# FFN up-projection by one Strassen step on token halves, in five passes of 512 tokens

## Chip, cores and metric

The kernel runs on one core of one Trainium2 chip. Its engines are TensorE (PE, matmuls and transposes into PSUM; its weight loads are listed as PEld), VectorE (DVE), ScalarE (ACT), GpSimd (POOL) and SyncE (SP, which issues nearly all DMAs). The metric is the device time of one execution in microseconds (us), as the median of several executions.

## What is computed

One layer of an encoder with parallel mixers, for a sample of 2048 tokens (`s`) and a prompt of 512 tokens (`p`), all in float32. The part that matters here is the feed-forward network (FFN) at its end:

```
h   = rms_norm(x2, norm2_g)                       # [L, 1024]
u   = dwconv3(h @ w_ffn_in, ffn_conv_w, ffn_conv_b)   # [L, 5632], width-3 convolution along the tokens
act = gelu(u[..., :2816]) * u[..., 2816:]         # gate part, up part
y   = x2 + act @ w_ffn_out
```

`x2` is the output of the mixers (attention, pooling, Hyena convolution) and of an output projection with its residual. To keep float32 accuracy on TensorE's faster float32r matmul, each operand is split in two: `hi`, the value rounded by a copy, and `lo`, the remainder. A product is then three matmuls: hi·hi, hi·lo, lo·hi (`mm3`, lines 323 to 325).

## The kernel before

The program has three stretches. First the projections of both batches run with the sample's mixers beside them, and then the sample's output projection (`front`). Then the FFN's up-projection (`ffn_in`) runs with the prompt's mixers beside its first part. Last comes the down-projection (`ffn_out`), with the halves of the weights `wo` that `wo_load` loaded before.

`ffn_in` is called three times: for the first 1024 tokens of the sample, for the 512 tokens of the prompt, and for the other 1024 tokens of the sample. Each call goes over 22 column tiles `f` of the gate part and the up part (`part` 0 and 1). For each part it loads 128 columns of weights (`fw`, 512 KB), splits them (`fwhi` on ACT, line 318; `fwlo` on DVE, line 319), and runs 8 x 3 matmuls of 512 tokens for each 512 tokens into one PSUM bank. ACT then writes the middle tap of the convolution with its bias from PSUM into `cv` (line 1322), and DVE adds the two other taps from PSUM (line 1312). Gelu is on ACT (line 1338), gate times up on DVE (line 1340), and SP stores the result to `act` in DRAM.

`ffn_prep` makes the FFN's input: row tiles of 128 tokens are loaded, normed (ACT, DVE, and a power on POOL, line 346), transposed on PE (line 357), and split into `hi` and `lo`.

`drive` writes two streams of instructions into one program: `main`, here `ffn_in`, and `side`, the mixers of the prompt and `ffn_prep` for the next part. A ratio says how much of the side stream goes with the main one. A scheduler then orders each engine's instructions; on the chip each engine runs its own in that order, and semaphores hold an instruction back until its inputs and buffers are there. In `run` the side stream is: the sample's mixers, its attention, `norm_s` (FFN input of the first half), then, once `front` has ended (`"up"`), the prompt's attention, pooling, Hyena and output projection, and the prompt's FFN input.

Of the kernel before, what the change touches and what calls it, by code (L numbers as in the profile page):

```python
# [32 lines left out]
class Seq:  # L33
    """One request batch: its length, its FFT split N = 64 * N2 and the derived tile counts."""
# [15 lines left out]
# the tables of 128 partitions that stay on chip: name and columns  # L50
# [5 lines left out]
def _shape_tables():  # L56
    """DFT matrices, positions, decays, distances: all from shapes alone."""
# [40 lines left out]
    # of the first four heads; those of the others are 1/16 of it  # L98
# [14 lines left out]
    for s in SEQS.values():  # L113
# [34 lines left out]
        # rows (b, ri, g, j), columns (ri, g, k2), block diagonal over g  # L148
# [13 lines left out]
        # positions of the forward filter and of the backward one, in the order (j, b, n1)  # L162
# [15 lines left out]
        # [b, n1, chunk, g, j, c']  # L178
# [15 lines left out]
def _arrays(inputs):  # L194
    """The arrays of the launch: the large inputs as they are, the small ones laid out by partition."""
# [35 lines left out]
RATIO_P = 0.4  # L231
# [10 lines left out]
class Trunk:  # L242
# [13 lines left out]
    def consts(self, c):  # L256
# [12 lines left out]
        self.edge = c.tile([128, 2, 2 * NF], F32, name="edge")  # L269
# [46 lines left out]
    def split(self, x, hi, lo):  # L316
        nc = self.nc
        self.keep(nc.scalar.activation(hi, x, AF.Copy))  # L318
        self.keep(nc.vector.tensor_tensor(lo, x, hi, op=ALU.subtract))  # L319

    def mm3(self, ps, lhi, llo, rhi, rlo, start, stop):
        nc = self.nc
        nc.tensor.matmul(ps, lhsT=lhi, rhs=rhi, start=start, stop=False)  # L323
        nc.tensor.matmul(ps, lhsT=lhi, rhs=rlo, start=False, stop=False)  # L324
        nc.tensor.matmul(ps, lhsT=llo, rhs=rhi, start=False, stop=stop)  # L325
# [12 lines left out]
    def norm(self, pool, g, x, n):  # L338
        """The first n rows of x after RMS norm with gain g, in place."""
# [10 lines left out]
    def norm_t(self, xn, n, hi, lo, c0, bank):  # L350
        """xn, transposed, to columns c0.. of hi and lo."""
# [13 lines left out]
    def front(self):  # L365
        """p of the sample, q, k and v of both, p of the prompt, then the sample's output projection behind its attention. The
        weights of a part take the place of those of the part before, tile by tile."""
# [5 lines left out]
        with tc.tile_pool(name="front", bufs=1, reuse_waits="tile") as pool:  # L373
# [16 lines left out]
            def fill(i, c0):  # L390
                """Weights i: columns c0.. of w_in, piece by piece."""
# [30 lines left out]
            def place(i):  # L422
                """Where row tile i goes, transposed: hi, lo and the column."""
# [32 lines left out]
            def also(it):  # L456
                """it, with the row tiles and the weights to come."""
# [54 lines left out]
            # the first tiles as they come; the weights last, for the next pool to start below them  # L512
# [1047 lines left out]
```

## Time and profile before

| | us |
|---|---|
| three runs | 3138.93, 3138.91, 3135.88 (median 3138.91) |
| span of the profiled execution | 3140.1 |
| from the first up-projection matmul to the first of the down-projection | 1144.9 to 2531.7 |
| from there to the end | 608.4 |

The profile is of one execution of its own; its time is given as its span, from the first to the last instruction, 1.2 us above the median of the runs. Rows of instruction groups read: line, engine, operation, output and inputs with their shapes, count, then busy time in us and the mean of one in ns, then the engine's idle time before them and who ended it. Matmuls overlap, so their pace is read from how far their starts are apart, not from their durations.

### The profile page before, as it was taken

What the parts mean: (1) busy time and instruction counts of PE and PEld (TensorE: products, weight loads), DVE (VectorE), ACT (ScalarE), POOL (GpSimd) and SP (SyncE); (2) the same over time, 40 slices, a digit from 0 to 9 for tenths busy, and PEclk for the clock granted to TensorE, in tenths of its full rate; (3) what the DMA queues carried; (4) which work ended last, traced back from release to release, by engine and by line L of the source; (5) the groups of instructions that cost most, each with busy time, mean ns of one, the idle gap of its engine ahead of it and who ended that gap; (6) DMA issues with size and microseconds to landing.
All of it is one profiled execution on the core that took longest, in us unless ns stands there. A gap on an engine that the chain in (4) does not pass through costs nothing.

```text
span 3140.1 us, 41553 instructions
## 1 busy us (share of the span) xinstructions
PE 3053.5 (97%) x15992; PEld 2556.1 (81%) x15992; DVE 1676.3 (53%) x3168; ACT 1173.7 (37%) x2021; POOL 210.5 (7%) x248
## 2 busy tenths in 40 slices
PE   7999999899999999999999999999999999999999
PEld 6887888888878877788887888888888888888887
DVE  7443567759998777666445565564444442111111
ACT  5222454448877546434223343332222231111110
POOL 1000000012233230000000000000000000000000
PEclk9999999999999999999999999999999999999999
DMA  5555586663533441454313243442222143223222
GB/s 178 151 152 138 163 230 170 178 176 100 152 100 94 145 138 61 131 166 133 98 63 128 89 137 118 127 142 67 74 67 74 54 131 111 74 77 101 74 75 77
DMA packets 399051, 369.94 MB, mean 118 GB/s; under 512 B 74937, under 2 KB 332857, under 8 KB 397829
## 3 DMA queue, kind: packets, MB, share of 16 engines
q1 hardware_dynamic: 395685, 356.64, 37.6%
q0 software_dynamic: 2880, 10.49, 0.8%
q8 instruction: 126, 2.06, 0.3%
q14 instruction: 72, 0.59, 0.1%
q10 hardware_dynamic: 288, 0.16, 0.0%
HBM read 278.08 MB, written 89.13 MB: 117 GB/s over the span
## 4 chain that ended last, share of the span: by engine, by line
PE 69%; DVE 5%; ACT 3%; DMA 2%; issue 1%; POOL 1%; SPq 0%; POOLq 0%; ACTq 0%; DVEq 0%
PE b L323 21%; PE b L325 21%; PE b L324 21%; PE b L1160 1%; PE b L1111 1%; ACT sb L1127 1%; PE b L1142 1%; PE b L1141 1%; PE b L865 1%; PE b L852 1%; DVE sb L1114 0%; PE b L357 0%; DVE nx L347 0%; DVE sb L1135 0%; DMA raw<-in_w_in_dram 0%
## 5 line engine op out<-in xcount | busy, mean ns | idle before, releaser
L323 PE MATMUL b<-h,fwhi 128*128 128x512 f32 x1408 | 562.5, 400 | 0.9 <-DVE x L1237 0.9
L325 PE MATMUL b<-h,fwlo 128*128 128x512 f32 x1408 | 560.0, 398 | 0.3 <-DVE fwlo L319 0.3
L324 PE MATMUL b<-h,fwhi 128*128 128x512 f32 x1408 | 559.0, 397 | 0.0
L1312 DVE SCALAR_TENSOR_TENSOR cv<-b,cst,cv 128x511 f32<-128x511 f32 (+1 forms) x616 | 351.8, 593 | 153.9 <-ACT cv L1322 147.3
L319 DVE TENSOR_TENSOR fwlo<-fw,fwhi 128x1024 fp32r<-128x1024 f32 x132 | 161.4, 1224 | 326.7 <-ACT fwhi L318 326.7
L325 PEld LDWEIGHTS b<-h,fwlo 128*128 128x128 f32 x1408 | 265.5, 189 | 64.5 <-DVE fwlo L319 0.8
L323 PEld LDWEIGHTS b<-h,fwhi 128*128 128x128 f32 x1408 | 265.8, 189 | 63.1 <-issue 1.8
L324 PEld LDWEIGHTS b<-h,fwhi 128*128 128x128 f32 x1408 | 265.7, 189 | 61.6
L319 DVE TENSOR_TENSOR al<-ar,ah 128x512 fp32r<-128x512 f32 x110 | 76.0, 691 | 420.4 <-ACT ah L318 420.4
L318 ACT ACTIVATE fwhi<-fw 128x1024 fp32r<-128x1024 f32 x132 | 139.8, 1059 | 387.9 <-PE b L324 385.1
L324 PE MATMUL b<-h,ah 128*128 128x512 f32 x640 | 249.2, 389 | 0.0
L323 PE MATMUL b<-h,ah 128*128 128x512 f32 x640 | 249.1, 389 | 0.0
L325 PE MATMUL b<-h,al 128*128 128x512 f32 x640 | 248.9, 389 | 0.0
L318 ACT ACTIVATE ah<-ar 128x512 fp32r<-128x512 f32 x110 | 69.4, 631 | 474.9 <-PE b L324 462.4
L1322 ACT ACTIVATE cv<-b,cst 128x512 f32<-128x512 f32 x220 | 169.2, 769 | 200.1 <-PE b L325 199.9
L323 PE MATMUL b<-W,h 128*128 128x256 f32 (+1 forms) x672 | 224.7, 334 | 2.1 <-ACT W L318 0.7
L324 PE MATMUL b<-W,h 128*128 128x256 f32 (+1 forms) x672 | 214.8, 320 | 0.7 <-DVE W L319 0.3
L325 PE MATMUL b<-W,h 128*128 128x256 f32 (+1 forms) x672 | 213.9, 318 | 0.0
L323 PE MATMUL b<-h,W 128*128 128x256 f32 x640 | 200.3, 313 | 3.4 <-ACT W L318 1.5
L325 PE MATMUL b<-h,W 128*128 128x256 f32 x640 | 184.5, 288 | 3.8 <-DVE W L319 3.8
L324 PE MATMUL b<-h,W 128*128 128x256 f32 x640 | 183.1, 286 | 0.0
L325 PEld LDWEIGHTS b<-h,al 128*128 128x128 f32 x640 | 120.1, 188 | 25.3 <-DVE al L319 0.2
(204 smaller groups left out, 5791.8 us busy)
## 6 DMA issues: line engine op xcount, KB each, us to landing
fw<-in_w_ffn_in_dram SPq DMA_DIRECT2D x132, 512.0 KB, 3.8
ar<-acts SPq DMA_DIRECT2D x88, 256.0 KB, 2.7
nx<-in_x_sample_dram SPq DMA_DIRECT2D x32, 512.0 KB, 4.4
tf<-in_t2f_s_dram SPq DMA_DIRECT2D x64, 256.0 KB, 3.3
acts<-cv SPq DMA_DIRECT2D x22, 512.5 KB, 2.6
raw<-in_w_in_dram SPq DMA_DIRECT2D x44, 256.0 KB, 3.1
rw<-in_w_ffn_out_dram SPq DMA_DIRECT2D x44, 256.0 KB, 2.7
acts<-cv SPq DMA_DIRECT2D x22, 511.5 KB, 3.1
```

The source lines that it names most:

```text
L318: self.keep(nc.scalar.activation(hi, x, AF.Copy))
L319: self.keep(nc.vector.tensor_tensor(lo, x, hi, op=ALU.subtract))
L323: nc.tensor.matmul(ps, lhsT=lhi, rhs=rhi, start=start, stop=False)
L324: nc.tensor.matmul(ps, lhsT=lhi, rhs=rlo, start=False, stop=False)
L325: nc.tensor.matmul(ps, lhsT=llo, rhs=rhi, start=False, stop=stop)
L852: nc.tensor.matmul(ps[:, i * C:i * C + C], lhsT=tf[:, i], rhs=x1[:, k0 + i], start=True, stop=True)
L865: nc.tensor.matmul(ps[:, i * C:i * C + C], lhsT=ti[:, i], rhs=t1[:, i * C:i * C + C], start=True, stop=True)
L1111: nc.tensor.matmul(ps[:, :nk], lhsT=qs[h][:, b * 128:b * 128 + 128], rhs=kk[:, ks], start=(i == 0), stop=(i == 1))
L1127: nc.scalar.activation(sc[h][:, :nk], sc[h][:, :nk], AF.Exp, bias=ng[:, h:h + 1], accum_out=den[:, h:h + 1])
L1141: nc.tensor.matmul(po, lhsT=v, rhs=phi, start=(i == 0), stop=False)
L1312: nc.vector.scalar_tensor_tensor(o, ps, taps[i], o if to is None else to, op0=ALU.mult, op1=ALU.add)
L1322: nc.scalar.activation(cv[:, a - o0:a - o0 + 512], ps, AF.Identity, scale=taps[1], bias=self.fcb[:, m:m + 1])
```

## The change

The up-projection runs in five passes of 512 tokens: four of the sample, then the prompt. In each pass one step of Strassen's algorithm (Winograd's form, with chains of sums) replaces each group of 2 x 2 block products. The blocks are: the first and second half of the 1024 input channels (the depth), the gate and the up columns of tile `f`, and the first and second 256 tokens. Instead of 8 products of half depth there are 7.

The token side is combined once for a pass, in `ffn_prep`: seven operands (`op` 0 to 6) of half depth and 256 tokens, each in `hi` and `lo`, from sums and differences on DVE and POOL. The weight side is combined for every tile `f` of every pass: four sums on POOL (`s12`, `s34`, 128x512 each), and four split groups, `g1` (the gate weights), `g2` (`s12`), `g3` (`s34`) and `g4` (half of the up weights). ACT makes all `hi`; DVE makes the `lo` of `g1` and `g2`, POOL that of `g3` and `g4`. Tile `f` of a pass is called a step below. The buffers of `g1` to `g3` (`fk`) are one set, so those of the next step can only be written when the products of this step have read them.

A step's products go in the order 1 to 7, each of 4 x 3 matmuls of 256 tokens, into four PSUM banks: 1 (`pa`, `g1`), 2 (`pb`, `g2`), 3 (`pd`, `g3`), 4 (`pc`, `g2`), and then 5 (`pa`, `g1`), 6 (`pd`, `g4`) and 7 (`pc`, `g3`), which add to what stands in their banks. Between them ACT copies `pa` to `u` (after 1 and after 5), and DVE makes partial sums `u2`, `u3` and the outputs in `u`, a tile in SBUF with one buffer. Product 5 must wait for the copy of `pa` after product 1, product 6 for `u3`, product 7 for the output from `pc`. The convolution then reads `u` instead of PSUM: middle tap on ACT, the two others as `scalar_tensor_tensor` on DVE (called taps below), gelu on ACT, and gate times up on POOL. The border tokens of two passes go through `edge`.

Beside this, the prompt's output projection loads its weights in two halves of 512 columns and prepares its input for each; the prompt's attention and the first pass's input `prep(0)` stand ahead of `"up"`; `RATIO_P` is 1.0 instead of 0.4; seven instead of eight row tiles of `w_ffn_out` fit each large tile.

```diff
-RATIO_P = 0.4
+RATIO_P = 1.0
+FT = 512
...
-        self.keep(nc.vector.tensor_tensor(lo, x, hi, op=ALU.subtract))
+        self.keep((engine or nc.vector).tensor_tensor(lo, x, hi.bitcast(F32), op=ALU.subtract))
...
+            def put(op, cs, x):
+                self.split(x, h[:, op, 0, :, cs], h[:, op, 1, :, cs], nc.gpsimd if op > 4 else None)
...
+                if i % 2 == 0:
+                    b = [pool.tile([128, 4, 128], F32, tag=f"b{j}", name=f"b{j}") for j in range(2)]
+                    for j in range(2):
+                        nc.scalar.activation(b[j], pv[j], AF.Copy)
+                        put(j, cs, pv[j])
+                else:
+                    nc.vector.tensor_tensor(t1, pv[0], b[0], op=ALU.subtract)
+                    nc.vector.tensor_tensor(t2, pv[1], t1, op=ALU.subtract)
+                    put(2, cs, pv[1])
+                    put(3, cs, t1)
+                    nc.gpsimd.tensor_tensor(b[0], t2, b[0], op=ALU.subtract)
+                    nc.gpsimd.tensor_tensor(b[1], b[1], t2, op=ALU.subtract)
+                    put(4, cs, t2)
+                    put(5, cs, b[0])
+                    put(6, cs, b[1])
...
+            a11, a12, a21, a22 = (x[:, k:k + 4] for x in ws for k in (0, 4))
+            s12, s34 = (pool.tile([128, KD, 128], F32, tag="fs", bufs=2, name="fs") for _ in range(2))
+            g1 = split(ws[0], "fk", 3)
+            nc.gpsimd.tensor_tensor(s12[:, 0:4], a21, a22, op=ALU.add)
+            nc.gpsimd.tensor_tensor(s12[:, 4:8], s12[:, 0:4], a11, op=ALU.subtract)
+            nc.gpsimd.tensor_tensor(s34[:, 0:4], a11, a21, op=ALU.subtract)
+            g2 = split(s12, "fk", 3)
+            nc.gpsimd.tensor_tensor(s34[:, 4:8], a12, s12[:, 4:8], op=ALU.subtract)
+            g3 = split(s34, "fk", 3, nc.gpsimd)
+            g4 = split(a22, "fl", 1, nc.gpsimd)
+            u = pool.tile([128, 2, FT + 4], F32, tag="u", bufs=1, name="u")
...
+            def add(o, ps, x):
+                nc.vector.tensor_tensor(o, ps[:, :N], x, op=ALU.add)
+
+            pa, pb, pd, pc = bank(), bank(), bank(), bank()
+            yield from product(pa, g1, 0, 0)
+            nc.scalar.activation(u[:, 0, lo], pa[:, :N], AF.Copy)
+            yield from product(pb, g2, 4, 4)
+            add(u2, pb, u[:, 0, lo])
+            yield from product(pd, g3, 0, 5)
+            add(u3, pd, u2)
+            yield from product(pc, g2, 0, 3)
+            add(u[:, 1, hi], pc, u3)
+            yield from product(pa, g1, 4, 1, False)
+            nc.scalar.activation(u[:, 0, lo], pa[:, :N], AF.Copy)
+            yield from product(pd, g4, 0, 6, False)
+            add(u[:, 1, lo], pd, u2)
+            yield from product(pc, g3, 4, 2, False)
+            add(u[:, 0, hi], pc, u2)
...
+                nc.scalar.activation(cv, u[:, part, c0:c0 + w], AF.Identity, scale=self.fcw[:, 1, m:m + 1], bias=self.fcb[:, m:m + 1])
+                for i in (0, 2):
+                    nc.vector.scalar_tensor_tensor(cv, u[:, part, c0 + i - 1:c0 + i - 1 + w], self.fcw[:, i, m:m + 1], cv,
+                                                   op0=ALU.mult, op1=ALU.add)
...
-            nc.vector.tensor_tensor(cvs[0], cvs[0], cvs[1], op=ALU.mult)
+            nc.gpsimd.tensor_tensor(cvs[0], cvs[0], cvs[1], op=ALU.mult)
...
-                     self.mark("c", "s"), pace(RATIOS[2]), self.attention(S, *att), norm_s(), self.need("up"), self.attention(P, *att),
+                     self.mark("c", "s"), pace(RATIOS[2]), self.attention(S, *att), self.attention(P, *att), prep(0), self.need("up"),
```

DVE in the up-projection, before (a stretch of the sample's second half; `b0` to `b4` are PSUM banks):

```order
L319 TENSOR_TENSOR fwlo_19637<-fw_19634,fwhi_19636 128x1024
L1312 SCALAR_TENSOR_TENSOR cv_19435<-b2_19466,cst_75,cv_19435 128x511 x2
L1312 SCALAR_TENSOR_TENSOR cv_19435<-b2_19466,cst_75,cv_19435 128x1
L1312 SCALAR_TENSOR_TENSOR cv_19435<-b1_19436,cst_75,cv_19435 128x1
L1312 SCALAR_TENSOR_TENSOR cv_19503<-b3_19504,cst_75,cv_19503 128x511 x2
```

DVE in one step of the second pass of the changed kernel (`fk_21273` and `fk_21280` are the `lo` of the next step's `g1` and `g2`):

```order
L1378 TENSOR_TENSOR u23_21156<-b1_21159,u_21155 128x256
L1378 TENSOR_TENSOR u23_21157<-b2_21160,u23_21156 128x256
L1378 TENSOR_TENSOR u_21155<-b3_21161,u23_21157 128x256
L320 TENSOR_TENSOR fk_21273<-fw_21266,fk_21272 128x1024
L320 TENSOR_TENSOR fk_21280<-fs_21270,fk_21279 128x1024
L1378 TENSOR_TENSOR u_21155<-b2_21160,u23_21156 128x256
L1378 TENSOR_TENSOR u_21155<-b3_21161,u23_21156 128x256
L1410 SCALAR_TENSOR_TENSOR cv_21255<-u_21155,cst_75,cv_21255 128x512
L1410 SCALAR_TENSOR_TENSOR cv_21260<-u_21155,cst_75,cv_21260 128x512
L1410 SCALAR_TENSOR_TENSOR cv_21255<-u_21155,cst_75,cv_21255 128x512
L1410 SCALAR_TENSOR_TENSOR cv_21260<-u_21155,cst_75,cv_21260 128x512
```

The taps took one operand from PSUM before; now both of their tiles, `u` and `cv`, lie in SBUF, and five sums of 256 columns from PSUM stand among them. In some steps beside the preparation of the next pass the `lo` of `g1` stands ahead of the second or third sum.

POOL in the up-projection had nothing before but powers and a few sums for the prompt's mixers and the norms. In the changed kernel this is what stands there for one step (`fs` are `s12` and `s34`, `fl` is `g4`):

```order
L1360 TENSOR_TENSOR fs_21270<-fw_21268 128x512
L1362 TENSOR_TENSOR fs_21271<-fw_21266,fw_21268 128x512
L1361 TENSOR_TENSOR fs_21270<-fs_21270,fw_21266 128x512
L1364 TENSOR_TENSOR fs_21271<-fw_21266,fs_21270 128x512
L1415 TENSOR_TENSOR cv_21118<-cv_21118,cv_21123 128x512
L320 TENSOR_TENSOR fl_21289<-fw_21268,fl_21288 128x512
L320 TENSOR_TENSOR fk_21285<-fs_21271,fk_21284 128x1024
```

Seven operations of two SBUF inputs a step came to POOL: the four sums for the next step, gate times up of the step before, and the `lo` of the next step's `g4` and `g3`.

ACT for the same step (`b0` is bank `pa`; `fk_21272`, `fk_21279`, `fl_21288`, `fk_21284` are the `hi` of the next step's `g1`, `g2`, `g4`, `g3`):

```order
L1383 ACTIVATE u_21155<-b0_21158 128x256
L1397 ACTIVATE u_21155<-edge_78 128x2x2
L319 ACTIVATE fk_21272<-fw_21266 128x1024
L319 ACTIVATE fk_21279<-fs_21270 128x1024
L1391 ACTIVATE u_21155<-b0_21158 128x256
L319 ACTIVATE fl_21288<-fw_21268 128x512
L319 ACTIVATE fk_21284<-fs_21271 128x1024
L1401 ACTIVATE edge_78<-u_21155 128x4
L1408 ACTIVATE cv_21255<-u_21155,cst_75 128x512
L1408 ACTIVATE cv_21260<-u_21155,cst_75 128x512
L1413 ACTIVATE cv_21255<-cv_21255 128x512
L1383 ACTIVATE u_21292<-b0_21295 128x256
```

The four `hi` of the next step stand between the copies of this one and its convolution; the next step's first copy of `pa` (last row) stands behind this step's gelu, and waits for all four taps, since they read the one buffer of `u`.

More of the change, by code (lines that the diff above doesn't have):

```diff
@@ L1256, in out_proj @@
-            yield from self.need((key, n))
-            for t in range(L // 128):
-                ts = slice(t * 128, t * 128 + 128)
-                ca = pool.tile([128, DM], F32, tag="ca", name="ca").rearrange("p (k t) -> p k t", k=KD)
-                nc.sync.dma_start(out=ca, in_=self.cat[n][:, ts].rearrange("(k p) t -> p k t", p=128))
-                x = pool.tile([128, DM], F32, tag="ox", name="ox")
-                nc.sync.dma_start(out=x, in_=src[ts, :])
-                sq, hi, lo = (pool.tile([128, KD, 128], dt, tag=nm, name=nm) for nm, dt in (("osq", F32), ("chi", F32R), ("clo", F32R)))
-                self.out_prep(ca, sq, hi, lo)
-                yield from self.until(self.now + T_NORM)
-                r = self.out_scale(pool, bank, sq, GROUPS)
-                yield from self.out_product(bank, hi, lo, x, r, GROUPS, wo)
-                nc.gpsimd.dma_start(out=self.x2[n][t * 128:t * 128 + 128, :], in_=x)
-                self.done.add(("x2", n, t))
@@ L1446, in big @@
         def big(pool):
-            return pool.tile([128, 2, KD * 1024], F32R, tag="h", name="h")
-        def hview(t):
-            return [t[:, i, :KD * 1024].rearrange("p (k t) -> p k t", k=KD) for i in range(2)]
+            return pool.tile([128, 7, 2, 4, FT // 2], F32R, tag="h", name="h")
         mc = self.ctx.enter_context(tc.tile_pool(name="mconst", bufs=1, side="right", reuse_waits="tile"))
@@ L1462, in run, with prep @@
         att = [att(i) for i in range(3)]
[L1463 to L1478 removed]
+        passes = [(S, t) for t in range(0, S.L, FT)] + [(P, t) for t in range(0, P.L, FT)]
+        pools, hs = [], {}
+        def prep(i):
+            if i < 2:
+                pools.append(self.ctx.enter_context(tc.tile_pool(name=f"h{i}", bufs=1, side="right", reuse_waits="tile")))
+            hs[i] = big(pools[i % 2])
+            yield from self.ffn_prep(passes[i][0], hs[i], passes[i][1], a)
+            self.done.add(("h", i))
         def consts():
@@ L1520, in load @@
         def load():
-            for f, v in enumerate(wviews(big(pb))):
+            po.append(self.ctx.enter_context(tc.tile_pool(name="ffo", bufs=1, side="right", reuse_waits="tile")))
+            for f, v in enumerate(wviews(big(pools[1]))):
                 self.wo_load(v, f, raw)
                 yield 4000
-        self.drive(self.ffn_in(S, pool, cvp, hB, 1024, 1024, self.rotate((0, 1, 2, 3, 4))), load(), 0.1)
-        wctx.close()
+        with tc.tile_pool(name="ffw", bufs=1, reuse_waits="tile") as pool:
+            for i, (s, t0) in enumerate(passes):
+                if i == 0:
+                    side = self.drive(self.ffn_in(s, pool, hs[0], t0, self.rotate((0, 1, 2, 3))), side, RATIO_P)
+                else:
+                    self.wo = {}
+                    ahead = prep(i + 1) if i + 1 < len(passes) else load()
+                    side = self.drive(self.ffn_in(s, pool, hs[i], t0, self.rotate((0, 1, 2, 3))), ahead, 0.1)
+                self.drive(side or (), None, 0)
```

211 lines of the change are left out of this document (105 added, 106 removed).

## The prediction

> **What bounds the kernel now.** I read the busy shares first, then the up-projection by windows, then single operations.
>
> ```profile
> PE 3053.5 (97%) x15992; PEld 2556.1 (81%) x15992; DVE 1676.3 (53%) x3168; ACT 1173.7 (37%) x2021; POOL 210.5 (7%) x248
> ...
> L323 PE MATMUL b<-h,fwhi 128*128 128x512 f32 x1408 | 562.5, 400 | 0.9 <-DVE x L1237 0.9
> L323 PE MATMUL b<-hp,fwhi 128*128 128x512 f32 x352 | 139.7, 397 | 0.0
> ...
> 1144.90:2531.70 1386.80, 1379.36 (x6171) 1116.13 (x6172) 764.13 (x1375) 495.76 (x694) 40.48 (x49) 1.00 0.33 102
> 2200.00:2300.00 100.00, 100.00 (x428) 80.40 (x427) 46.76 (x85) 26.98 (x32) 0.00 (x0) 1.00 0.22 71
> ```
>
> TensorE bounds it. In the up-projection (third row: busy time of PE, weight loads, DVE, ACT, POOL; then clock, DMA share, GB/s) PE has work for 1379 of 1387 us, DVE for 55%, ACT for 36%, POOL for 3%. The pace: 428 matmuls of 512 tokens in 100 us, 0.2336 us each. There are 3 x (1408 + 352) = 5280 of them, so 1233 us; the other 154 us are PE work of the prompt's mixers and of the norms beside it.
>
> **What the change can save.** It needs 5 passes x 22 steps x 7 products x 12 = 9240 matmuls of 256 tokens. The trace has that shape in the input projection:
>
> ```profile
> 101.70 0.28 PE L325 MATMUL b<-h,W 128*128 128x256 f32 x1
> ...
> 102.78 0.28 PE L325 MATMUL b<-h,W 128*128 128x256 f32 x1
> ```
>
> Nine matmuls later the start is 1.08 us later: 0.12 us each, weight load hidden. A product is 12 x 0.12 = 1.44 us, a step 10.1 us, all 110 steps 1109 us. So 124 us, 4% of the kernel, is the most that PE gives.
>
> **What a step asks of the other engines.** Durations:
>
> ```profile
> L318 ACT ACTIVATE fwhi<-fw 128x1024 fp32r<-128x1024 f32 x132 | 139.8, 1059 | 387.9 <-PE b L324 385.1
> L318 ACT ACTIVATE ah<-ar 128x512 fp32r<-128x512 f32 x110 | 69.4, 631 | 474.9 <-PE b L324 462.4
> ...
> L507 ACT ACTIVATE o<-b 128x256 f32<-128x256 f32 x20 | 7.6, 381 | 5.3 <-PE b L325 5.1
> ...
> L319 DVE TENSOR_TENSOR fwlo<-fw,fwhi 128x1024 fp32r<-128x1024 f32 x132 | 161.4, 1224 | 326.7 <-ACT fwhi L318 326.7
> L802 DVE SCALAR_TENSOR_TENSOR hst<-hst,mcst 128x512 f32<-128x512 f32 x12 | 8.8, 737 | 3.8 <-ACT hst L799 3.6
> L926 DVE TENSOR_TENSOR zg<-b,zg 128x256 f32<-128x256 f32 x16 | 5.8, 400 | 0.0
> ...
> L1054 POOL TENSOR_TENSOR kn<-kt,hr 128x512 f32<-128x512 f32 x6 | 6.2, 1040 | 0.5
> L1059 POOL TENSOR_TENSOR qn<-qt,hr 128x1024 f32<-128x1024 f32 x20 | 38.8, 1942 | 53.4 <-issue 26.8 <-PE b L1086 25.1 <-POOL hr L1013 0.7
> ```
>
> DVE: two `lo` of 1.22, four taps of 0.74, five sums of 0.40: 7.4 us. POOL: six operations of 512 at 1.04 and one of 1024 at 1.90 (its duration undisturbed, below): 8.1 us. ACT: three `hi` of 1.06, one of 0.63, two copies of 0.38, and about 2.4 for convolution, gelu and edges: 7.0 us. Each is below 10.1, so by sums alone PE would stay the bound. They are not independent, though:
>
> ```profile
> 782.39 0.69 DVE L319 TENSOR_TENSOR W<-raw,W 128x512 fp32r<-128x512 f32 x1
> ...
> 783.47 2.34 DVE L319 TENSOR_TENSOR W<-raw,W 128x512 fp32r<-128x512 f32 x1
> ...
> 781.63 1.64 POOL L1013 TENSOR_TENSOR hr<-hss,mhalf 128x8 f32<-128x8 f32 x1 [21.52 <-DMA raw<-in_w_in_dram]
> 783.36 1.90 POOL L1059 TENSOR_TENSOR qn<-qt,hr 128x1024 f32<-128x1024 f32 x1
> ...
> 789.80 0.75 DVE L581 SCALAR_TENSOR_TENSOR W<-raw,cst,W 128x512 fp32r<-128x512 f32 x1
> ...
> 790.47 0.95 DVE L581 SCALAR_TENSOR_TENSOR W<-raw,cst,W 128x512 fp32r<-128x512 f32 x1
> ...
> 789.93 0.95 POOL L1209 TENSOR_TENSOR osq<-osq 128x128 f32<-128x128 f32 x1
> ...
> 790.84 0.91 POOL L1209 TENSOR_TENSOR osq<-osq 128x128 f32<-128x128 f32 x1
> ...
> 1487.99 0.75 DVE L1237 SCALAR_TENSOR_TENSOR ox<-b,or,ox 128x512 f32<-128x512 f32 x1 [1.87 <-PE b L325]
> ...
> 1487.15 2.00 POOL L1209 TENSOR_TENSOR osq<-osq 128x256 f32<-128x256 f32 x4
> ```
>
> (Start and duration in us, engine, operation.) The same DVE subtraction takes 0.69 us, and 2.34 when POOL's wide multiplication has begun 0.11 us before it: it ends at 785.81, 0.55 behind POOL's 785.26. So **a DVE operation with two inputs in SBUF and a POOL operation on SBUF exclude each other**. The next four rows show the turns: the POOL sum of 789.93 ends at 790.88, 0.33 behind the first DVE operation; the second DVE operation ends 0.54 behind that; the second sum 0.33 behind that. Where both have work queued, they alternate. In the last two rows the DVE operation reads PSUM and one SBUF tile, beside a running series of POOL sums, and keeps its 0.75 us.
>
> The Trainium skill, page "SBUF — State Buffer", section "Who interferes with whom", states that two SBUF inputs on DVE contend with a GpSimd reader and that the loser waits for the whole instruction. The trace agrees for wide operations; 782.39 stayed at 0.69 us inside a power of 1.64 us on eight columns, so I count the time of reading only. By whole instructions a step would hold 8.1 + 5.4 = 13.5 us, about the loop that I find below, so the sum hardly hangs on it.
>
> Before, the taps read PSUM, and POOL was idle. Now both `lo`, the four taps and all seven POOL operations are of the kind that excludes. Counted behind a release: taps 0.54, `lo` about 1.08, POOL 0.92 and 1.8 (0.12 less, as 0.33 is less than the 0.45 of a free 128-column sum): 4 x 0.54 + 2 x 1.08 + 6 x 0.92 + 1.8 = 11.6 us a step, above PE's 10.1.
>
> **The loop.** By the order of ACT, DVE and POOL, a step is tied to the one before, from the end of its product 5 to that of the next:
> - ACT, in order, for the next step's weights: `g1` 1.06 and `g2` 1.06, the second copy of `pa` 0.38, `g4` 0.63, `g3` 1.06: 4.19 us (`g1` waits for product 5, `g3` for product 7, which has ended by then).
> - POOL: the `lo` of `g4` holds it 0.2 us more, then the `lo` of `g3`: 1.90.
> - Meanwhile the convolution's first tap is ready and waits; then tap, sum, tap, sum, tap, sum, tap, as POOL's four sums are queued there: 0.54 + 3 x (0.92 + 0.54) = 4.92.
> - Only now may ACT write the one buffer `u`: 0.38. Product 5 waits for this copy: 1.44.
> - Some six handovers of 0.05: 0.3.
>
> Sum: 4.19 + 2.1 + 4.92 + 0.38 + 1.44 + 0.3 = **13.3 us a step**. PE stands idle for 3.2 us of it, mostly ahead of product 5. The weights' DMA does not come into it:
>
> ```profile
> fw<-in_w_ffn_in_dram SPq DMA_DIRECT2D x132, 512.0 KB, 3.8
> ```
>
> The second weight tile of the next step is asked for when `g1`'s `lo` is done, and lands 3.8 us later, about when POOL comes to the sums; 1 MB per 13.3 us is 79 GB/s.
>
> **The other terms.**
>
> ```profile
> 307.10:310.60 3.50, 1.59 (x13) 1.42 (x13) 0.37 (x1) 0.00 (x0) 0.00 (x0) 1.00 0.83 254
> 310.60:314.05 3.45, 3.45 (x19) 3.45 (x18) 0.00 (x0) 0.80 (x2) 0.00 (x0) 0.51 0.43 139
> ...
> 1156.20:1159.60 3.40, 0.98 (x8) 0.69 (x7) 3.12 (x7) 0.67 (x2) 2.70 (x3) 1.00 0.36 101
> 1159.60:1163.00 3.40, 3.13 (x15) 2.28 (x14) 2.74 (x6) 2.52 (x4) 2.40 (x2) 1.00 0.45 130
> ...
> 800.00:900.00 100.00, 96.68 (x595) 82.25 (x594) 91.84 (x244) 85.02 (x199) 29.63 (x25) 1.00 0.40 118
> ...
> L1160 PE MATMUL b<-cst,sb x448: 270/272/332, 714.8 to 1279.3; 128*128 128x128 f32 x150
> ...
> L325 PE MATMUL b<-owhi,clo 128*128 128x512 f32 x64 | 25.5, 399 | 0.0
> ```
>
> - *Clock.* After 1.9 idle of 3.5 us the granted clock was 0.51 for the next 3.4 us. After 2.4 idle of 3.4 us at 1156 it stayed 1.00. The gap ahead of product 5 is longer than both, so I take a quarter of 110 gaps at 1.4 us (product 5 at half speed): 40 us, bounds 0 and 150. The Trainium skill, page "TensorE: Matmul & The Clock Gate", section "Why this matters for your kernels", says that gaps up to about 3 us keep the clock. The trace differs, with 0.51 behind 1.9 us; by the page the sum would be 40 us less.
> - *First pass.* The prompt's pooling, Hyena and output projection (3 x 64 matmuls of 0.2336, 45 us of PE) run beside it. They were at most the 154 us above; PE's idle time hides part, while they also use DVE and POOL: 80, bounds 0 and 154.
> - *Input of the next pass, weights of the last.* Four preparations add about 8 us of DVE and 11 us of POOL that exclude each other; 14 splits of `wo` add 10 us: 60, bounds 0 and 100.
> - *Order.* In 18 steps a `lo` stands ahead of a sum that product 6 or 7 waits for, 2.4 or 1 us late: 25, bounds 0 and 45.
> - *Start.* The prompt's attention moves ahead of the first up-projection matmul, with its DMAs and its POOL operations, beside the last sample tiles of the output projection. DVE is at 92% where the sample's attention runs. Now it runs between 1144.9 and 1279.3 (last row but one), so at most 134 us come ahead, at least none, if it fits beside those tiles: 40, nearer to none, since PE work of the output projection is there to run beside it.
> - The down-projection keeps its 608 us: 7 weight tiles ahead of it instead of 8 last 7 x 5.5 = 38 us, and the rest arrive faster than that.
>
> Sum: 110 x 13.3 = 1463, + 40 + 80 + 60 + 25 = 1668 instead of 1387: +281; +40 at the start: **+321**, 3140 to 3461; against the median, 1 us less. I take 3460.
>
> **The rivals.**
> 1. *Exclusion without strict turns.* POOL's sums come late or DVE's taps go in a row; the loop shrinks to what the exclusion itself needs, 11.7 us: 110 x 1.6 = 176 less, **3285**. For it: the second weight tile lands only just in time. Against it: the turns at 789.80.
> 2. *No bound but PE*, the other side: the taps on `u` do not wait for POOL. The loop then fits into PE's 10.1 plus 0.4 for product 3, which waits for `g3`: 110 x 10.5 + 115 for the rest = 1270, -117 + 40: **3060**. It decides in favour of the change below 12 us a step. Against it: 783.47.
> 3. *The clock falls at every gap*: 110 x 1.6 instead of 40, **3600**. For it: the row at 310.60; against it: the row at 1159.60.
> 4. *The saving is eaten up exactly*, within 0.2%: a step of about 11 us, between 1 and 2.
>
> **How the numbers follow.** Forecast 62%, rival 1 18%, rival 2 8%, rival 3 10%, rival 4 2%. The likeliest is 3460, by its own bounds 3350 to 3570. The range 3250 to 3640 takes in rivals 1 and 3 and leaves out 2 and 4. Faster by over 0.2% (about what a measurement of this kernel can tell from none) 8%, within 2%, slower 90%.
>
> **What would show it.** Steps of 13 us in the middle passes, PE at about 76% there; product 5 waiting for ACT's copy, and behind it the taps; taps of 1.4 to 1.7 us instead of 0.74, POOL sums of 1.5 instead of 1.04, taking turns; `lo` of `g3` ending late for product 3; a clock below 1 in some slices. Taps of 0.74 beside running POOL sums would prove the loop wrong, and so would a PE that is busy all the time.

## The result, and the profile after

| | before | after |
|---|---|---|
| median of four runs | 3138.88 us (3135.88 to 3138.93) | 3755.29 us (3751.53 to 3760.84) |
| profiled execution, span | 3140.1 | 3749.7 |
| first matmul of the up-projection | 1144.9 | 1205.1 |
| up-projection, first to last matmul | 1387 | 1933 |
| from there to the end | 608 | 611 |

The ratio is **1.196, 95% interval 1.194 to 1.198**: 616 us slower. The direction was as predicted, but 3755 lies outside the range of 3250 to 3640. Nearly all of the difference is in the up-projection: 546 us, where 281 were forecast.

The page of the changed kernel: busy time by engine, the granted clock in 40 slices, and the groups that cost most (busy us, mean ns of one | idle time before them and who ended it).

```profile
PE 3195.3 (85%) x19976; PEld 2885.1 (77%) x19976; DVE 2462.3 (66%) x3530; ACT 1561.0 (42%) x2785; POOL 1582.5 (42%) x1082
...
PEclk9999999999998989988888888898888889999999
...
L325 PE MATMUL b<-h,fk 128*128 128x256 f32 x2640 | 818.0, 310 | 266.3 <-ACT u L1383 260.1
L327 PE MATMUL b<-h,fk 128*128 128x256 f32 x2640 | 809.3, 307 | 127.6 <-POOL fk L320 119.0
L1410 DVE SCALAR_TENSOR_TENSOR cv<-u,cst,cv 128x512 f32<-128x512 f32 (+2 forms) x440 | 780.8, 1830 | 122.9 <-ACT cv L1408 122.6
...
L320 POOL TENSOR_TENSOR fk<-fs,fk 128x1024 fp32r<-128x1024 f32 x110 | 275.2, 2502 | 68.6 <-ACT fk L319 64.1
```

PE falls from 97% to 85% busy, and its matmuls look busier than they are (below). It waits in the two places that the prediction named: 260 us for ACT's copy into `u` (product 5), and 119 us for POOL's `lo` of `g3` (product 3). The taps take 1.83 us instead of 0.74. New is the clock: 17 of the 22 slices of the up-projection (slices 13 to 34) have an 8, 0.80 to 0.89, where the kernel before had 1.00 over its up-projection. By windows (us; PE, weight loads, DVE, ACT, POOL; clock), first pass, then the next three, then the last:

```profile
1205.10:1707.00 501.90, 399.80 (x2632) 372.47 (x2632) 392.64 (x481) 226.73 (x355) 323.30 (x226) 0.89 0.42 126
1707.00:2810.00 1103.00, 831.92 (x5624) 801.80 (x5624) 853.60 (x814) 470.95 (x777) 823.09 (x496) 0.85 0.29 87
2810.00:3138.00 328.00, 252.50 (x1717) 243.34 (x1718) 252.62 (x277) 133.55 (x192) 230.43 (x139) 0.85 0.28 85
```

A step, measured from one gelu (L1413) to the next, takes 16.2 us on average in the undisturbed steps 6 to 20 of passes 2 to 4. The forecast was 13.3. One of them, in the timeline (start, duration, engine, line; several DVE operations of one kind are one row):

```profile
2603.76 1.29 POOL L320 TENSOR_TENSOR fl<-fw,fl 128x512 fp32r<-128x512 f32 x1 [4.19 <-ACT fl L319]
...
2604.96 1.06 ACT L319 ACTIVATE fk<-fs 128x1024 fp32r<-128x1024 f32 x1 [1.27 <-PE b L326]
...
2606.10 2.39 POOL L320 TENSOR_TENSOR fk<-fs,fk 128x1024 fp32r<-128x1024 f32 x1 [1.04 <-ACT fk L319]
2606.77 7.34 DVE L1410 SCALAR_TENSOR_TENSOR cv<-u,cst,cv 128x513 f32<-128x513 f32 x4 [1.32 <-ACT cv L1408]
2608.45 1.74 POOL L1360 TENSOR_TENSOR fs<-fw 128x512 f32<-128x512 f32 x1
2610.16 1.73 POOL L1362 TENSOR_TENSOR fs<-fw 128x512 f32<-128x512 f32 x1
2611.84 1.72 POOL L1361 TENSOR_TENSOR fs<-fs,fw 128x512 f32<-128x512 f32 x1
2613.64 1.60 POOL L1364 TENSOR_TENSOR fs<-fw,fs 128x512 f32<-128x512 f32 x1
2614.22 0.38 ACT L1383 ACTIVATE u<-b 128x256 f32<-128x256 f32 x1 [1.12 <-DVE cv L1410]
```

This is the predicted loop, in the predicted order: `lo` of `g3`, then four taps and POOL's sums in turns, then the copy. The first tap starts at 2606.77, while POOL's `lo` runs, and ends only at 2609.04, 0.55 us after it (2608.49), as the wide subtraction did in the prediction's rows. What follows on PE, its matmuls and the windows around them:

```profile
2614.66 0.58 PE L325 MATMUL b<-h,fk 128*128 128x256 f32 x1 [3.26 <-ACT u L1383]
2615.04 0.41 PE L326 MATMUL b<-h,fk 128*128 128x256 f32 x1
2615.25 0.41 PE L327 MATMUL b<-h,fk 128*128 128x256 f32 x1
...
2617.67 0.28 PE L327 MATMUL b<-h,fl 128*128 128x256 f32 x1
2617.78 0.28 PE L325 MATMUL b<-h,fl 128*128 128x256 f32 x1
```

```profile
2609.00:2612.40 3.40, 2.40 (x21) 2.19 (x19) 3.40 (x4) 0.00 (x0) 3.40 (x3) 1.00 0.00 0
2612.40:2615.80 3.40, 1.14 (x5) 1.14 (x6) 2.72 (x6) 2.05 (x4) 3.32 (x3) 0.75 0.00 0
2615.80:2619.20 3.40, 3.40 (x25) 3.40 (x24) 2.39 (x3) 1.61 (x3) 0.68 (x1) 0.75 0.28 92
2619.20:2622.60 3.40, 3.40 (x32) 3.40 (x31) 1.75 (x4) 2.57 (x4) 2.38 (x2) 1.00 0.64 168
```

PE stands idle for 3.26 us, and behind it product 5 starts a matmul every 0.213 us instead of every 0.118, until 2617.5. PE counts as busy all that time; only the clock column and the distance of the starts show it.

### The profile page after: what moved, and what is told of

Read it like the earlier page. It is cut to its first block, busy times and chain, and to the rows that moved or that the text cites. A ratio compares the mean times of both kernels' runs of the same rounds, so it can differ in the third digit from the quotient of the medians.

```text
span 3749.7 us, 53187 instructions
## 1 busy us (share of the span) xinstructions
PE 3195.3 (85%) x19976; PEld 2885.1 (77%) x19976; DVE 2462.3 (66%) x3530; ACT 1561.0 (42%) x2785; POOL 1582.5 (42%) x1082
## 4 chain that ended last, share of the span: by engine, by line
PE 30%; DVE 17%; issue 5%; ACT 5%; POOL 3%; DMA 2%; ACTq 0%; SPq 0%; DVEq 0%; POOLq 0%
DVE cv L1410 16%; PE b L325 10%; PE b L326 10%; PE b L327 9%; ACT cv L1408 2%; ACT fk L319 1%; DMA rw<-in_w_ffn_out_dram 1%; ACT u L1383 1%; POOL fk L320 0%; POOL fs L1364 0%; DVE h L320 0%; POOL h L320 0%; POOL fl L320 0%; POOL cv L1415 0%; DMA raw<-in_w_out_dram 0%
## 5 line engine op out<-in xcount | busy, mean ns | idle before, releaser
L325 PE MATMUL b<-h,fk 128*128 128x256 f32 x2640 | 818.0, 310 | 266.3 <-ACT u L1383 260.1
L327 PE MATMUL b<-h,fk 128*128 128x256 f32 x2640 | 809.3, 307 | 127.6 <-POOL fk L320 119.0
L1410 DVE SCALAR_TENSOR_TENSOR cv<-u,cst,cv 128x512 f32<-128x512 f32 (+2 forms) x440 | 780.8, 1830 | 122.9 <-ACT cv L1408 122.6
L326 PE MATMUL b<-h,fk 128*128 128x256 f32 x2640 | 797.9, 303 | 0.0
L325 PEld LDWEIGHTS b<-h,fk 128*128 128x128 f32 x2640 | 560.3, 212 | 291.2 <-ACT u L1383 278.7
L327 PEld LDWEIGHTS b<-h,fk 128*128 128x128 f32 x2640 | 558.2, 212 | 150.0 <-POOL fk L320 139.7
L326 PEld LDWEIGHTS b<-h,fk 128*128 128x128 f32 x2640 | 559.6, 212 | 2.3 <-issue 0.5
L1378 DVE TENSOR_TENSOR u<-b,u 128x256 f32<-128x256 f32 x550 | 231.5, 422 | 164.1 <-PE b L327 108.3
L319 ACT ACTIVATE fk<-fs 128x1024 fp32r<-128x1024 f32 x220 | 232.9, 1058 | 250.8 <-PE b L326 236.5
L320 POOL TENSOR_TENSOR fk<-fs,fk 128x1024 fp32r<-128x1024 f32 x110 | 275.2, 2502 | 68.6 <-ACT fk L319 64.1
L320 POOL TENSOR_TENSOR fl<-fw,fl 128x512 fp32r<-128x512 f32 x110 | 153.5, 1396 | 354.8 <-ACT fl L319 335.7
L1413 ACT ACTIVATE cv<-cv 128x512 f32<-128x512 f32 (+2 forms) x110 | 69.3, 630 | 495.7 <-DVE cv L1410 495.5
L325 PE MATMUL b<-h,ah 128*128 128x512 f32 x560 | 218.4, 390 | 0.9 <-ACT ah L319 0.8
L326 PE MATMUL b<-h,ah 128*128 128x512 f32 x560 | 218.1, 389 | 0.0
L1360 POOL TENSOR_TENSOR fs<-fw 128x512 f32<-128x512 f32 x110 | 183.9, 1672 | 49.1 <-DMA fw<-in_w_ffn_in_dram 31.9
```

Source lines behind the costliest of these rows:

```text
L320: self.keep((engine or nc.vector).tensor_tensor(lo, x, hi.bitcast(F32), op=ALU.subtract))
L1360: nc.gpsimd.tensor_tensor(s12[:, 0:4], a21, a22, op=ALU.add)
L1378: nc.vector.tensor_tensor(o, ps[:, :N], x, op=ALU.add)
L1410: nc.vector.scalar_tensor_tensor(cv, u[:, part, c0 + i - 1:c0 + i - 1 + w], self.fcw[:, i, m:m + 1], cv, op0=ALU.mult, op1=ALU.add)
L1413: nc.scalar.activation(cv, cv, AF.Gelu)
```

## The experiments

Each was run once, beside a run of the kernel before on the same chip (3131 to 3136 us), so differences of a few us say nothing. "Step" is the mean of steps 6 to 20 of passes 2 to 4; "first pass" the mean step there, from its first gelu to the first of the second pass; "tap" the busy time of one tap in 2300 to 2600 us (busy time over count; neighbours overlap a little, so the mean duration of one is up to 0.06 us longer).

| | us | first pass | step | tap | clock, 2300 to 2600 |
|---|---|---|---|---|---|
| changed kernel | 3755 | 21.4 | 16.2 | 1.85 | 0.86 |
| e1_u1 | 3580 | 20.6 | 13.8 | 1.63 | 0.94 |
| e2_p4x3 | 3652 | 21.8 | 14.2 | 1.75 | 0.97 |
| e10_p4x2 | 3651 | 21.4 | 14.6 | 1.84 | 0.97 |
| e11_u1_p4x2 | 3578 | 21.1 | 13.7 | 1.63 | 0.97 |
| e4_sums_dve | 3491 | 19.0 | 14.2 | 0.98 | 0.95 |
| e6_u1_sums_dve | 3467 | 19.0 | 13.4 | 1.15 | 0.96 |
| e3_nosums | 3283 | 18.3 | 11.3 | 1.09 | 0.99 |
| e7_u1_nosums | 3238 | 17.3 | 10.8 | 1.07 | 0.98 |
| e12_sums_dram | 3261 | 19.0 | 10.7 | 1.06 | 0.99 |
| e5_att_behind | 3763 | 24.4 | 16.2 | 1.83 | 0.85 |

### The clock: product 4 twice and three times

The same product is computed again into the same bank, so PE has 1.44 or 2.88 us more to do ahead of its gap (e10_p4x2, e2_p4x3).

```diff
-            yield from product(pc, g2, 0, 3)
+            for _ in range(3):
+                yield from product(pc, g2, 0, 3)
```

> Product 4 is run three times into its bank (the same values each time), which adds 24 matmuls, 2.9 us, to the 10.1 us of PE in a step, and puts them into the gap ahead of product 5. Clock theory (the gap halves the clock for products 5 and 6, which lie in the loop): the granted clock goes from 0.85 to nearly 1 in the middle passes, a step from 16.1 to about 13.9 us, the kernel to about 3510 us although PE has more to do. Rival (the halved clock lies beside the loop): the step stays at 16.1 us, 3750 us, or grows.

> The changed kernel with product 4 run twice (once for a result that is overwritten), so that PE has 1.44 us more work in each step ahead of product 5 and its gap there shrinks by as much. Theory (the half clock follows from the length of the gap; with the product three times the step fell from 16.1 to 14.2 us): part of the half clock goes, steps of 14.2 to 15.2 us, granted clock 0.90 to 0.97 in the middle passes, 3650 to 3710 in all. Rival (the clock was not the cause, and the third run of the product moved something else): steps of 16 us or more, clock 0.86.

PE's waits in 2300 to 2600 us (total, times, longest), changed kernel, then product 4 twice:

```profile
PE b L325 <- ACT u L1383: 48.2, 16, 3.3
```

```profile
PE b L325 <- ACT u L1383: 33.3, 18, 1.9
```

More work makes the kernel 100 us *faster*. Twice is enough: the mean gap falls from 3.0 to 1.85 us, most steps take 14.2 us, some 15.7. Measured from product 5 to product 5 in steps 6 to 20 of passes 2 to 5, 42 of 60 steps have no time at half clock and take 14.2 us, and 17 have one stretch of 3.4 us and take 15.7. In the changed kernel each of these 60 has 2.8 to 6.7 us at half clock. It has two steps (the sixth of passes 4 and 5) with none at all, and they take 14.17 us behind the usual gap. So 14.2 is the loop without the half clock, and the half clock costs the other 2.0 us.

The matmuls at half pitch (0.19 to 0.24 us apart instead of 0.118) lose 1.9 us a step in passes 2 to 5 of the changed kernel, and 0.73 with product 4 twice. The difference, 1.2, is about what the steps of passes 2 to 4 gain on average (16.7 to 15.6 us, with the steps beside a preparation as slow as before). The first pass gains nothing, so the whole falls by 104 us, half of 110 x 2.0. With the product three times the step came out near the expected 13.9, but the whole missed the expected 3510 by 142 us for the same reason.

### The buffer `u`: a tile of its own for the first copy

```diff
-            nc.scalar.activation(u[:, 0, lo], pa[:, :N], AF.Copy)
+            u1 = pool.tile([128, N], F32, tag="u1", bufs=2, name="u1")
+            nc.scalar.activation(u1, pa[:, :N], AF.Copy)
             yield from product(pb, g2, 4, 4)
-            add(u2, pb, u[:, 0, lo])
+            add(u2, pb, u1)
```

> The copy of the bank after product 1 goes to a tile of its own (u1) instead of u, so that product 5 no longer waits for the four taps; the sums u2 and u3, and with them product 6, still stand behind the taps on DVE. Theory (turns of DVE and POOL in a loop through u, lengthened by a halved clock behind PE's gap): the loop loses the copy and product 5, a middle step goes from 16.1 to about 14.0 us, the kernel to about 3520 us; taps still take some 1.8 us. Rival (the copy of pa is no part of the loop; POOL's own sum of work sets the step): no change, 3750 us.

> The copy after product 1 in a tile of its own, and product 4 run twice: PE has 11.5 us of work a step. Exclusion theory (the 13.6 us of the separate tile alone are what DVE and POOL need when they exclude each other, and PE's gaps and clock do not matter any more): 13.4 to 13.8 us a step again, 3570 to 3600 in all, with a higher clock. Rival (the rest above 11.5 is still PE at half clock in its gaps): 12 to 13 us a step, 3500 or less.

Product 5 waits for `u` no more; the step falls to 13.6 in most cases (28 of the 45 counted), and the next wait in line is product 6 for `u3`, whose DVE sum stands behind the taps (in 2300 to 2600 us):

```profile
PE b L325 <- DVE u L1378: 39.7, 17, 6.0
```

The taps still take 1.63 us. The whole, 3580, lies 60 us above the expected 3520. Filling PE's gap as well changes nothing: 13.7, 3578 us. So with `u` out of the way another bound stands at 13.6. DVE and POOL show it (e11_u1_p4x2; columns as above):

```profile
2300.00:2600.00 300.00, 257.66 (x1991) 245.01 (x1990) 270.34 (x261) 142.77 (x227) 261.28 (x153) 0.97 0.33 100
```

DVE is busy for 270 of 300 us and POOL for 261. Undisturbed, a step's operations take 7.4 us on DVE and 9.9 on POOL (six of 1.26 and one of 2.34), so about 162 and 217 us of the 300; much of the rest is time in which one waits for the other. That this sets the 13.6 is argued from these numbers; the runs without sums on POOL, below, bear it out. The loop through `u` cost only 0.6 us above this, 14.2 against 13.6, besides the clock.

### The sums: on DVE, left out, or made once

e4_sums_dve moves the four weight sums from POOL to DVE; e6_u1_sums_dve does that with the separate tile.

```diff
-            nc.gpsimd.tensor_tensor(s12[:, 0:4], a21, a22, op=ALU.add)
+            nc.vector.tensor_tensor(s12[:, 0:4], a21, a22, op=ALU.add)
...
```

> The four sums go from POOL to DVE; nothing is left out. Theory: DVE has 2.8 us more to do in a step (10.2 us), but the taps stand behind sums of 0.7 us of their own engine instead of POOL's of 1.15 to 1.3 us; a step takes about 13.6 us, the kernel about 3475 us, taps 0.74 us. Rival (DVE is the engine that lacks time, and POOL helps it): slower than 3750 us.

> Both single edits together: the copy after product 1 in a tile of its own, and the four weight sums on DVE; nothing is left out. Exclusion theory: with the sums off POOL, what excludes each other in a step is DVE's two lo (2.4), four taps (2.9) and four sums (2.8) and POOL's lo of g3 (2.3), lo of g4 (1.3) and product (1.3): 13.0 less the part of POOL's that needs no port, so 12 to 13 us a step, about 3390 to 3430 in all. Rival (a step is a loop through u and the half clock, and both single edits cut the same loop): the step falls no further than with the separate tile alone, 13.5 us, 3490.

In the next two the sums are made only in the first step of each pass, and the other 21 steps use those; this part of the computation is left out.

```diff
+            if f == 0:
                 nc.gpsimd.tensor_tensor(s12[:, 0:4], a21, a22, op=ALU.add)
...
```

> The four sums of the weights on POOL are made for the first step of each pass only; all other steps split the sums of that first step, so the up-projection is not the reference's. Theory (DVE's taps and POOL's sums exclude each other in turns): taps fall from 1.83 to about 0.74 us, the four of a step from 7.3 to 3 us behind the lo of g3, the gap of PE shrinks below 2 us and the clock stays up, a step takes about 11 us, the kernel about 3200 us. Rival (taps of two SBUF inputs with a shifted read are slow by themselves): taps stay at 1.8 us, the step loses nothing, 3750 us.

> The copy in a tile of its own, and the weight sums made only in the first step of each pass; the other 21 steps use those, so the output is not the reference's. It shows what the seven products bring when nothing but them and the splits is left. Theory: steady steps of 10.1 to 10.7 us at full clock (product 3 still waits half a microsecond for POOL's lo of g3), PE busy for 95% and more in the middle passes; the whole is 3210 to 3240, still slower than before, by the later start and a first pass of 17 to 18 us a step. Rival (some further cost lies in the products themselves, so that 256 tokens a matmul do not run at 0.12 us each): steps of 11 us and more with PE busy.

In 2300 to 2600 us: the taps with the sums on DVE (e4_sums_dve), then the window and PE's longest wait without sums and with the separate tile (e7_u1_nosums):

```profile
L1410 DVE SCALAR_TENSOR_TENSOR cv<-u,cst,cv 128x513 f32<-128x513 f32 x84 | 82.1, 1012 | 11.2 <-ACT cv L1408 11.1
```

```profile
2300.00:2600.00 300.00, 279.05 (x2248) 272.78 (x2247) 248.57 (x353) 179.22 (x262) 142.72 (x84) 0.98 0.43 132
```

```profile
PE b L327 <- POOL fk L320: 16.7, 27, 2.1
```

With no sums on POOL the taps fall to about 1.0 or 1.1, so the sums beside them were most of what stretched them; the 0.74 expected is not reached, since the `lo` of `g3` and `g4` and the product stay on POOL. On DVE the sums take 264 us off the whole, and the first pass falls from 21.4 to 19.0, but a steady step still takes 14.2 us (13.6 expected), as long as the changed kernel's without the half clock: DVE has more to do, and POOL's `lo` is still in its way. With the separate tile too it is 13.4, just above the 12 to 13 expected, and 3467 us, above the 3430 expected. Without sums the step is 11.3, without the loop through `u` 10.8. What is left there, 0.6 us a step, is product 3 waiting for POOL's `lo` of `g3`; otherwise PE runs its 10.1. The seven products do bring what PE's matmul rate promised.

The total without sums alone missed on the high side (3283 for 3200), for the first pass, still 18.3 us a step, did not fall with the others.

The last one leaves nothing out: separate tile, sums once on DVE in the first pass, stored to DRAM and loaded in the others.

```diff
+            if not first:
+                for i, s_ in enumerate((s12, s34)):
+                    nc.sync.dma_start(out=s_, in_=self.sums[f][i].rearrange("p (k f) -> p k f", k=KD))
...
+                for i, s_ in enumerate((s12, s34)):
+                    nc.gpsimd.dma_start(out=self.sums[f][i].rearrange("p (k f) -> p k f", k=KD), in_=s_)
```

> Nothing is left out: the copy after product 1 in a tile of its own, and the weight sums made once, on DVE in the first pass, stored to DRAM, and loaded again in passes 2 to 5 (1.75 MB of weights a step there instead of 1). Theory (the sums' place beside the taps was the cost, and the loads fit: 1.75 MB in 10.7 us is 164 GB/s): first pass 19 to 20 us a step as with both single edits together, then 10.7 to 12 us, 3270 to 3330 in all; still slower than before, since even without any sums it was 3238. Rival (the loads come late: POOL's lo of g3 frees the buffer of s34 only late in a step, 3.8 us before the next can land): steps of 13 us and more with product 3 waiting, 3400 and more.

```profile
2300.00:2600.00 300.00, 280.27 (x2288) 274.28 (x2287) 248.57 (x359) 182.18 (x268) 138.86 (x81) 0.99 0.65 204
```

10.7 us a step at 204 GB/s, and 3261 us in all, 495 less than the changed kernel and a little below the 3270 expected. It is the best of the versions that leave nothing out, and still 4.1% slower than the kernel before beside it (3131): its up-projection starts 60 us later (1204.8), and lasts 1442.5 us instead of 1387. At 10.7 the 110 steps need 1177 us. The first pass, 19.0 us a step, adds 22 x 8.3 = 183, and the first five steps of the other passes, 11 to 18 us each beside the preparation of the next input, most of the rest. The kernel before had 154 us for all such work, since DVE and POOL had room for it.

### The start: the prompt's attention moved back

```diff
-  self.attention(S, *att), self.attention(P, *att), prep(0), self.need("up"),
+  self.attention(S, *att), prep(0), self.need("up"), self.attention(P, *att),
```

> The changed kernel with the prompt's attention moved back behind the start of the up-projection (the order before). Theory (the later start of 60 us is the prompt's attention, which found no cover ahead of the up-projection): the first up-projection matmul comes at 1150 to 1165 instead of 1205, and the first pass, whose steps wait for DVE and POOL in any case, grows by part of it: 30 to 50 us; the whole 3735 to 3755. Rival (the start is late through the seven token operands of the first input, which POOL and DVE make ahead of it): the first matmul stays at 1190 or later, and the whole does not fall.

The first up-projection matmul comes at 1140.2: the late start was the attention, all of it. But the up-projection grows by 78 us, to 2011.5, more than the 30 to 50 expected of the first pass, and nothing is won. In the kernel before the same attention ran under PE's work; here it has a price in either place.

### The control: POOL sums in the kernel before

Four POOL sums for each weight tile, from SBUF into a tile that nothing reads (e8_before_poolsums); then the same with one column repeated as second input (e9_before_bcast).

```diff
+                for _ in range(4):
+                    z = pool.tile([128, 4, 128], F32, tag="z", bufs=1, name="z")
+                    nc.gpsimd.tensor_tensor(z, w[:, 0:4], w[:, 4:8], op=ALU.add)
```

> The kernel before, with four sums of 128x512 on POOL added for every weight tile of the up-projection, from SBUF and into a tile that nothing reads. Its taps read PSUM. Exclusion theory: the taps on DVE keep 0.74 us beside running POOL sums, the lo of the weights (two inputs in SBUF) grows from 1.22 to 2 us and more, POOL's sums take 1.1 to 1.3 us, and the whole stays within 0.5% of before, since PE waits for none of it. Rival (a busy POOL slows every DVE operation, from PSUM too): taps of 1.2 us and more; then even these reach PE, and the whole is over 1% slower.

> The kernel before with the same four POOL sums of 128x512 for each weight tile as in the last run of it, but with one column repeated for the second input. Theory (the prediction's price of 1.04 us came from rows with a repeated operand; two whole inputs cost 1.26 to 1.29): these sums take 1.04 us undisturbed instead of 1.26. Rival (the price is by the count of elements, and 1.26 is what a busy DVE makes of it): 1.25 us again.

The added sums, then the taps from PSUM (`b`), then the border taps of one column whose two inputs lie in SBUF (`edge`, `cv`); ns, min/median/max:

```profile
L1308 POOL TENSOR_TENSOR z<-fw x528: 1257/1292/2282, 1137.2 to 2552.2; 128x512 f32<-128x512 f32 x176
...
L1315 DVE SCALAR_TENSOR_TENSOR cv<-b,cst,cv x616: 199/745/754, 1150.6 to 2601.4; 128x511 f32<-128x511 f32 x110, 128x1 f32<-128x1 f32 x44
...
L1315 DVE SCALAR_TENSOR_TENSOR cv<-edge,cst,cv x44: 211/486/1144, 2120.4 to 2595.3; 128x1 f32<-128x1 f32 x44
```

The same without the sums, in the kernel before:

```profile
L1312 DVE SCALAR_TENSOR_TENSOR cv<-b,cst,cv x616: 204/744/754, 1153.3 to 2535.0; 128x511 f32<-128x511 f32 x110, 128x1 f32<-128x1 f32 x44
...
L1312 DVE SCALAR_TENSOR_TENSOR cv<-edge,cst,cv x44: 208/213/218, 2045.4 to 2528.9; 128x1 f32<-128x1 f32 x44
```

And with the repeated column (e9_before_bcast):

```profile
L1308 POOL TENSOR_TENSOR z<-fw x528: 1038/1052/2121, 1142.3 to 2511.6; 128x512 f32<-128x512 f32 x176
```

This separates two things. A tap that reads PSUM and one SBUF tile never notices POOL: 754 ns is the longest with and without, although 232 of the 440 wide ones lay beside an added sum for more than 0.6 us. A tap of a single column with two SBUF inputs goes from at most 218 ns to as much as 1144. So it is the second SBUF input that makes DVE wait, not a busy POOL. The Trainium skill, page "SBUF — State Buffer", section "Who interferes with whom", has it so: a DVE instruction with at most one SBUF input, outside its 2-port modes, does not contend.

The `lo` of the weights, which has two SBUF inputs, bears this out in part: the 72 that met no added sum stay at 1.2 to 1.3 us, and the 60 that met one take 1.2 to 2.3, median 1.65; 2 us and more was expected.

And a POOL sum of two whole inputs takes 1.26 us, with a repeated one 1.04. The Trainium skill, page "GPSIMD Engine Reference", section "3.1 Elementwise — side-by-side cycle accounting", puts the price of two inputs down to one read port that serves both in turn, and measured 4497 ns for 2048 columns, so 1.12 us for 512 as an estimate. The measured 1.26 us is above that, and that a repeated column is cheaper speaks for the reason given; no run here shows the port itself.

One part of the expectation fell. e8_before_poolsums was to stay within 0.5% and took 3208 us, 2.4% more; with the repeated column it is 3168, 1.0% more. PE's waits in its up-projection, the largest of them (us in total, times, longest):

```profile
PE b L357 <- DVE nx L347: 12.0, 6, 2.9
PE b L1086 <- POOL qn L1059: 9.5, 1, 9.5
...
PE b L323 <- DVE cv L1315: 6.2, 1, 6.2
PE b L1072 <- POOL kn L1054: 5.5, 1, 5.5
```

The two longest that name POOL are for side work there, and the largest total is for a norm that has a power on POOL; both must now queue behind the sums. In the kernel before no wait of PE in its up-projection was over 2.4 us. Waits and clock together account for the loss: PE's idle time in the up-projection grows from 8 to 61 us, and its time at half clock from 7 to 55 us, which costs half of the 48 us more. That is 53 + 24 = 77 us, where the up-projection grew by 75.

## Why the prediction was wrong

By its own steps:

- **What bounds the kernel** was right. PE bounded it before. Afterwards it is the loop that the prediction drew: product 5 waits for ACT's copy, the copy for the taps, the taps for POOL. e1_u1 cuts the link to the copy, and PE's wait moves on to `u3`; e4_sums_dve takes the sums out of the turns, and the wait for the copy falls from 48.2 to 26.4 us in 2300 to 2600 us.
- **The loop of 13.3 us a step** had the right mechanism and too low a price for POOL. Without the half clock it is 14.2. The prices 1.04 and 1.90 came from rows whose operands are broadcast; two whole inputs take 1.26 and 2.34 (the shortest `lo` of `g3`). In the turns a tap and a sum take 1.7 us together where 1.46 was put in. In the 42 steps of e10_p4x2 without half clock, taps and sums behind the `lo` of `g3` take 5.6 us instead of 4.92, and this `lo` 2.4 instead of 1.9; the small terms came out 0.3 shorter. 110 x 0.9 = 100 us.
- **The clock** is the term that failed. The prediction had it happen at a quarter of the gaps, at 1.4 us each: 40 us. Of the 88 steps in passes 2 to 5, 73 had PE idle for 3.0 to 3.5 us ahead of product 5, and 70 of these had matmuls at half pitch behind it: 50 from product 5's start on, 20 from a later matmul of products 5 to 7. The price was too low as well: the half clock goes on past product 5 into 6, so that product 7 ends late and `g3` is split late (the row at 2604.96: ACT waited 1.27 us for PE), and the loop's next link starts late. 110 x 2.0 = 220 us instead of 40. Rival 3, which had the clock fall at every gap at 1.6 us each, had this step right and was given 10%. The row at 1159.60, with the clock at 1.00 behind 2.4 us idle, misled. The clock changes only at the borders of stretches of 3.41 us (last section), and those 2.4 us lay across such a border: 0.67 us before 1157.14 and 1.75 behind it. The 1.9 us of the other row lay in one stretch, 307.22 to 310.64, and the next one was at half clock.
- **First pass**: 22 x (21.4 - 16.2) = 114, forecast 80, within its bounds. **Preparations and order**: what is left, 1933 - 110 x 16.2 - 114 = 37, forecast 85. **Start**: 60, forecast 40, also within its bounds; e5_att_behind confirms the cause. **Down-projection**: 611, forecast 608.

Together: 100 + 180 for loop and clock, 34 for the first pass, less 48, 20 for the start, 3 at the end: 289 us, against the 290 between 3460 and the profiled 3749.7. That the sum closes shows nothing, as preparations and order are taken as what is left. The two large terms were measured by themselves: 280 us, both in the same direction. The clock alone would have ended at 3640, the upper end of the range; with the loop's price it lies beyond.

The signs that the prediction named came, and larger: taps of 1.83 us instead of 1.4 to 1.7, POOL sums of 1.6 to 1.7 instead of 1.5. That PE is busy for 75% of the middle passes, 76% being forecast, is luck: its 10.1 us are 62% of a step of 16.2, and the half pitch fills the rest.

Rival 1 (turns that are not strict) and rival 2 (taps that don't wait) are ruled out by the timeline of the step and by the taps of 1.83 us; rival 4, a step of about 11 us, falls with them. By e3_nosums, rival 2 would not have ended at 3060 either: with no sum on POOL it is 3283, because the first pass and the start remain.

Where did Strassen's saving go? e7_u1_nosums holds the answer: its steps of 10.8 us are shorter than the same share of the kernel before (1233 us over 110, 11.2), and yet the whole is about 100 us slower. Against the profiled kernel before it is 96: 59 are the later start and 36 the longer up-projection, whose first pass takes 17.3 us a step. Before, DVE had 45% and POOL 97% of the up-projection free, and the prompt's mixers, the norms and the splits ran there. In e7_u1_nosums DVE has 17% and POOL 52% free in 2300 to 2600 us. That this lack of room is what makes the first pass slow is argued; no run tests it alone.

## What to carry to other kernels

Fewer matmuls save only what the slowest engine pays: before PE's work is traded for sums on DVE and POOL, add up those of their operations that read two SBUF operands as if the two engines were one, at the price of two whole operands (here 5.4 + 9.9 = 15.3 us, an upper estimate: 13.6 to 14.2 were measured), and count the side work that now loses its cover. Where a new loop leaves PE idle for 3 us in every turn, price the turn at half clock, not as an accident; PE's busy time won't show it, the clock column and the distance of matmul starts do. Operands that are the same in every pass can be made once and loaded again if the DMA has room, as it had here (87 GB/s before that, 204 with it).

## What the runs showed of the hardware

**Gaps and the clock.** In all 14 profiles the granted clock is 1.00 or 0.50, and changes only at the borders of stretches of 3.41 us. What counts is PE's idle time within one stretch. The stretches at full clock, in all profiles together:

| PE idle in the stretch | stretches | next stretch at half clock |
|---|---|---|
| under 1.5 us | 12405 | 15 |
| 1.5 to 1.9 us | 326 | 84 |
| 1.9 us and more | 477 | 447 |

At half clock less is enough to stay there: of 293 such stretches with 0.7 us idle or more, all were followed by another one at half clock. So the length of a gap decides only together with its place. A gap of 3.0 to 3.5 us brought half pitch in 70 of 73 cases (changed kernel), one of 1.5 to 2.0 us in 23 of 82 (product 4 twice). The Trainium skill, page "TensorE: Matmul & The Clock Gate", section "Why this matters for your kernels", advises against gaps over about 3 us; here 1.9 us in one stretch was enough, so the measured figure is the one to go by.

- **More matmuls, less time.** 1.44 us of useless products in each step made the kernel 104 us faster.
- **One repeated column** as second operand makes a POOL sum of 128x512 17% shorter (1.04 for 1.26 us).
- **One column can wait for a whole sum**: the DVE tap of 128x1 took up to 1144 ns beside POOL sums of 1.26 us, and 213 without.
